# Block sums and early residual additions by accumulating transfers, and one seven-product pair of chunks in the first down pairs

## The chip, the cores and the metric

The kernel runs on one core of a Trainium2 chip. The metric is the device time of one execution in microseconds, as the median of several runs. The engines of the core are called here as the profile calls them: TensorE (PE), VectorE (DVE), ScalarE (ACT), GpSimd (POOL) and SyncE (SP). SP, ACT and POOL each have a queue from which they start DMA transfers.

## What is computed

A decoder trunk of two layers on 256 tokens of width 2048, all in float32. Layer 0 mixes tokens with gated linear attention, layer 1 with forgetting attention; both also attend to 256 memory tokens. The change touches the channel mixer, which each layer has after its attention, and two masks of the gated linear attention. The channel mixer of the reference:

```python
HIDDEN = 5632

def conv_ffn(h, w_up, conv_w, conv_b, w_down):
    u = causal_dwconv(h @ w_up, conv_w, conv_b)
    a, val = split_cols(u, [HIDDEN, HIDDEN])
    return (jax.nn.silu(a) * val) @ w_down

# in each layer, after the attention:
h = rmsnorm(x, norm_ffn[i])
x = x + conv_ffn(h, w_up[i], conv_w[i], conv_b[i], w_down[i])
```

## The kernel before

**Splitting.** A float32 matrix product is made of three fast products: each operand is split into a rounded high part (`whi`, made by ACT) and the rest (`wlo`, high part subtracted by VectorE), and hi·hi, hi·lo and lo·hi are added in PSUM. Weights arrive in units of 128 x 1024 floats (512 KB) on SP's queue into one of four `raw` buffers (`split_unit`, L212); `whi` and `wlo` have four buffers each. Activations (`h`, `m`) lie in SBUF already split, one buffer for each chunk of 128 rows.

**Pairs.** `pair_steps` (L351) multiplies all 256 tokens (two blocks of 128) by 1024 columns (two halves of 512) over n chunks. For one chunk that is 4 block products of 3 matmuls, 12 matmuls of 128 x 512, into four PSUM banks p2, p3, p4 and x. Some pairs of neighbouring chunks k, k+1 are done with **seven** block products instead of eight (Strassen's scheme in Winograd's form): 21 matmuls instead of 24. For those the tokens' sums stand ready (`token_sums`, L429; `usum`, `dsum`), and sums of the neighbouring weight blocks are needed: the two units come into `ra` and `rb` (tag raw2, two buffers), VectorE makes four sums of 128 x 512 (L397 to L400), and `split_more` (L342) casts four pieces w1 to w4 (512, 1024, 1024 and 1024 columns). Three more banks, p1, p5, p6 and p7, collect the products that several results share; after the last seven of a pair, `early` adds these into the results, and after the last unit `late` adds p2, p3, p4 and x.

**Channel mixer.** `ffn` (L330) works in parts of 16, 16 and 12 chunks of the hidden width (`PARTS`). *Up pairs* (11 in each layer, 16 units each) have a seven at chunk 6 (`SEVEN_UP`). Their `early` (L1417) puts the shared sums, scaled by the norm, into four temps; their results are turned from tokens to columns by a transpose on VectorE, a transfer to DRAM and four back on POOL's queue (`far_away`, L601). After a due time of 8 units (`turn(j, wait)`, L1386) the convolution's taps (ACT), their sums (VectorE), Silu and the product follow, two or fewer of these steps after each unit (`tick`). *Down pairs* multiply one part's gated chunks by 1024 of the 2048 output columns: f=0 for columns 0 to 1023 (x[0], x[1]), then f=2 (x[2], x[3]). In the first two parts both have sevens at chunks 4 and 10 (`SEVEN_DOWN`), so 8 sevens in each layer. A part's down pairs run after the first up pair of the next part. In the third part there are no sevens in the down product. The residual x lies in SBUF; `early` of a down pair (L1286) adds into it with one ACT and eight VectorE operations, four of which are additions to x (`add_to`, L453).

**Order.** A scheduler orders each engine's instructions by a simulated time line; `high_priority(offset=AHEAD)` lets an instruction be taken as if it stood 300 instructions earlier, which is how weights are loaded and split ahead. `issue_after` fixes an order by hand: all weight loads follow one another on SP's queue.

Of the kernel before, what the change touches and what calls it, by code (L numbers as in the profile page):

```python
# [20 lines left out]
P = 128  # L21
T = 256
# [13 lines left out]
SEVEN_DOWN = (4, 10)  # L36

# [107 lines left out]
def _trunk(ctx: ExitStack, tc: tile.TileContext, xt, xtok, memt, wp, wgu, gns, gfin, cnv, par, msk, out):  # L145
# [13 lines left out]
    mask = const.tile([P, M_N], F32, name="mask")  # L159
# [3 lines left out]
    scanmask = mask[:, M_SCAN : M_SCAN + T]  # L163
# [187 lines left out]
    def pair_steps(units, src, sums, flip, pool, early, late):  # L351
# [32 lines left out]
        places = (("p2", 0, 0), ("p3", 0, 1), ("p4", 1, 0), ("x", 1, 1))  # L384
        for k in plan:
            if k in sums:
                with tc.high_priority(offset=AHEAD):
                    ra, rb = [pool.tile([P, NUNIT], F32, name="raw2", tag="raw2", bufs=2) for _ in range(2)]
                    with tc.issue_after(loads[-1].ins):
                        for t, (off, _, w) in ((ra, units[k]), (rb, units[k + 1])):  # L390
                            loads.append(nc.sync.dma_start(t, wp[off : off + P * w].rearrange("(p n) -> p n", p=P)))
                st = [[sums[k][:, part, j, :] for part in range(2)] for j in (3, 0, 1, 2)]
                done = k == end[-1]
                w1 = split_more(ra[:, :512], 512)
                w2 = split_more(rb, 1024)
                with tc.high_priority(offset=AHEAD):
                    V.tensor_tensor(ra[:, :512], ra[:, 512:], ra[:, :512], ALU.subtract)  # L397
                    V.tensor_tensor(ra[:, 512:], rb[:, 512:], ra[:, 512:], ALU.subtract)
                    V.tensor_tensor(rb[:, 512:], rb[:, 512:], ra[:, :512], ALU.subtract)
                    V.tensor_tensor(rb[:, :512], rb[:, :512], rb[:, 512:], ALU.subtract)  # L400
# [12 lines left out]
                k += 1  # L413
            else:
                w = split_unit(units[k])
                last = k == n - 1
                steps = [(low, *place) for low in range(2) for place in places]
                if last:
                    steps.sort(key=lambda t: places.index(t[1:]))
                for low, name, b, h in steps:  # L420
                    for part in range(2 - low):
                        r = mm(name, tok(k, b)[part], w[low][:, h * 512 : (h + 1) * 512], last and low == 1)
                    if last and low:
                        ends.append(r)
                        late(b, h, bank[name])
                last_mm.append(r)
            yield k

    def token_sums(r, dst):  # L429

        t = r.rearrange("p s (b n) -> p (s b) n", b=2)
        a11, a21, a12, a22 = (t[:, n, :] for n in range(4))
        V.tensor_tensor(a22, a21, a22, ALU.add)
        V.tensor_tensor(a21, a11, a21, ALU.subtract)
        V.tensor_tensor(a11, a22, a11, ALU.subtract)
        V.tensor_tensor(a12, a12, a11, ALU.subtract)
        halves([dst[:, part] for part in range(2)], t)
# [272 lines left out]
    with tc.tile_pool(name="load", bufs=1) as lp:  # L710
# [57 lines left out]
        for u in range(8):  # L768
            step(u)
            if u == 1:  # L770
                squares()
            elif u == 3:
                for b in range(2):
                    S.activation(mv[0][:, b, :], mv[0][:, b, :], AF.Copy, scale=nrm.col()[:, b : b + 1])
                with tc.issue_after(loads[-1].ins):
                    for i in range(KC):
                        nc.sync.dma_start(xf[i], xt[i])
                    nc.sync.dma_start(part, par)
                    nc.sync.dma_start(mask[:, M_FOX:], msk[:, M_FOX:])
# [20 lines left out]
    def gla(nx):  # L800
        h, mix = bufB, bufA
        with tc.tile_pool(name="gla", bufs=1) as gp:
            scratch[0] = gp

# [28 lines left out]
            def gates(hd):  # L833
# [7 lines left out]
                for c in range(2):  # L841
# [11 lines left out]
                    V.tensor_tensor_scan(bc[:, c, :], scanmask, mz, 0.0, ALU.mult, ALU.add)  # L853
# [110 lines left out]
            def core(hd):  # L964
# [36 lines left out]
                eye = mask[:, M_EYE:].bitcast(I32).unsqueeze(1).to_broadcast(ins.shape)  # L1001
                V.copy_predicated(ins, eye, ps[:, 192:320].rearrange("p (b t) -> p b t", b=2))
                for li, B in enumerate(LEVELS):
                    H = B // 4
                    p3 = levels[li].rearrange("p (b c) -> p b c", b=2)
                    m3 = mask[:, M_LVL + NVER * li : M_LVL + NVER * (li + 1)].bitcast(I32)
# [276 lines left out]

    def down_pair(l, p, f, src, sums, flip, pool, temps, then=None):

        def early(bank):  # L1286
            t0, t1 = temps()
            S.activation(t0, bank["p1"], AF.Copy)
            add_to(f)(0, t0)
            V.tensor_tensor(t0, bank["p6"], t0, ALU.add)  # L1290
            V.tensor_tensor(t1, bank["p7"], t0, ALU.add)
# [38 lines left out]
    def ffn(l, nx, h, m, ys, zs, landing, then, pool, temps, spare=None, last=None):  # L1330
        with tc.tile_pool(name=f"ffn{l}", bufs=1) as fp:
# [79 lines left out]
            def up_pair(j):  # L1411

                count[2] += 1
                turns = [turn(j + 2 * h_, 8) for h_ in range(2)]
                u = {}

                def early(bank):  # L1417
                    u.update({(b, h_): temps(2 * b + h_) for b in range(2) for h_ in range(2)})
                    S.activation(u[0, 1], bank["p1"], AF.Copy)
                    S.activation(u[0, 0], bank["p1"], AF.Copy, scale=scale(0))  # L1420
                    V.tensor_tensor(u[0, 1], bank["p6"], u[0, 1], ALU.add)
                    V.tensor_tensor(u[1, 0], bank["p7"], u[0, 1], ALU.add)
                    V.tensor_tensor(u[0, 1], bank["p5"], u[0, 1], ALU.add)
                    V.tensor_tensor(u[1, 1], bank["p5"], u[1, 0], ALU.add)
                    for b, h_ in ((0, 1), (1, 0), (1, 1)):
# [22 lines left out]
            for p, (lo, hi) in enumerate(PARTS[:-1]):  # L1448
# [15 lines left out]
            wide = down_pair(l, p, 0, src, {}, 0, pool, lambda: (temps(0), temps(1)), then)  # L1464
# [61 lines left out]
    with tc.tile_pool(name="stash", bufs=1) as st:  # L1526
# [4 lines left out]
        with tc.tile_pool(name="turn1", bufs=1) as tp:  # L1531
            n2, then = preparing("kv", bufB, tp, dram, turned3, "raw2")
            ys = [const.tile([P, 4, 4, 2, 32], F32, name="yu", tag=tag) for tag in ("mk0", "mv0")]
            fixed = [vt.rearrange("p b t -> p (b t)")[:, 2048 + 512 * i : 2560 + 512 * i] for i in range(2)]

            def temps(i):
                return fixed[i] if i < 2 else tp.tile([P, 512], F32, name="temp", tag=f"temp{i}")
# [17 lines left out]
    with tc.tile_pool(name="store", bufs=1) as op:  # L1555
# [11 lines left out]
        def temps(i):  # L1567
            return op.tile([P, 512], F32, name="temp", tag=f"temp{i}")
# [116 lines left out]
```

## Time and profile before

| | us |
|---|---|
| median of 3 runs | 2282.79 |
| lowest, highest | 2279.04, 2285.32 |
| the profiled execution | 2282.04 |
| its span, first to last instruction | 2280.0 |
| TensorE busy | 2229.1 |
| VectorE busy | 1806.4 |
| ScalarE busy | 1421.8 |
| GpSimd busy | 127.0 |
| mean granted TensorE clock | 0.994 |

The matmuls of layer 0's channel mixer start at 457.6 us of the span, those of layer 1's at 1528.2. Rows of the profile name the line, the engine, the operation and the tiles (out<-in). A helper's line stands for all its calls, so L455 is every addition to x, and L229 and L348 are all splits. Tiles carry the name of the buffer that they lie in: `fvt` and `temp` are temps of the mixer, `mix`, `A`, `B` and `more` hold gated chunks, `yu` and `yzu` results on their way to being turned, `far` their place in DRAM. "PEld" is the load of a matmul's stationary operand.

### The profile page before, as it was taken

How to read it: one execution, taken by the hardware profiler on the slowest of the kernel's cores; microseconds unless marked ns; L12 is line 12 of the kernel's file. 1: busy time of each engine (PE TensorE's matmuls, PEld its weight loads, DVE VectorE, ACT ScalarE, POOL GpSimd, SP SyncE). 2: the span in 40 equal slices, each digit the busy share in tenths (PEclk: the TensorE clock that was granted, in tenths of full speed). 3: DMA queues.
4: the chain of work that ended last, by engine and by line, in shares of the span. 5: the costliest groups of instructions: out<-in, count | busy, mean ns of one | idle time of the engine just before them, and what ended most of it. 6: DMA issues, size and time to landing. Idle time of an engine off the chain costs nothing.

```text
span 2280.0 us, 30080 instructions
## 1 busy us (share of the span) xinstructions
PE 2229.1 (98%) x10311; PEld 1852.6 (81%) x10311; DVE 1806.4 (79%) x2667; ACT 1421.8 (62%) x2264; POOL 127.0 (6%) x239
## 2 busy tenths in 40 slices
PE   9999999999999999999999999999999999999997
PEld 7888888888887878778777998888787787878876
DVE  7768987688898878897777569677889878889776
ACT  6655665557776566764665455456776656775465
POOL 0000000001010001100100000000001001100010
PEclk9999999999999999999999999999999999999998
DMA  9866657876675667756678667676777556765674
GB/s 351 247 221 213 206 180 254 249 249 216 235 243 193 211 220 250 246 179 218 227 230 265 209 205 251 204 246 226 235 249 236 202 195 231 239 221 204 225 233 133
DMA packets 167170, 515.48 MB, mean 226 GB/s; under 512 B 20700, under 2 KB 43880, under 8 KB 167016
## 3 DMA queue, kind: packets, MB, share of 16 engines
q1 hardware_dynamic: 151080, 464.51, 62.1%
q0 software_dynamic: 15360, 48.25, 6.8%
q8 instruction: 81, 1.33, 0.2%
q10 hardware_dynamic: 576, 0.79, 0.1%
q14 instruction: 73, 0.60, 0.1%
HBM read 469.68 MB, written 43.79 MB: 225 GB/s over the span
## 4 chain that ended last, share of the span: by engine, by line
PE 75%; issue 11%; DVE 4%; ACT 4%; DMA 4%; POOL 1%; SPq 0%; ACTq 0%; DVEq 0%; POOLq 0%
PE acc L372 22%; PE acc L332 21%; PE ps_s L372 11%; PE ps_o L372 6%; PE ps_t L372 5%; PE acc L259 3%; PE acc L304 3%; PE ps_s L332 2%; PE acc L257 1%; DMA yzu<-far 1%; DMA raw<-wp 1%; ACT whi L228 1%; DVE wlo L229 1%; DVE wlo L348 1%; DMA fvt<-far 1%
## 5 line engine op out<-in xcount | busy, mean ns | idle before, releaser
L229 DVE TENSOR_TENSOR wlo<-raw,whi 128x1024 fp32r<-128x1024 f32 (+4 forms) x730 | 860.9, 1193 | 328.4 <-ACT whi L228 308.2
L228 ACT ACTIVATE whi<-raw 128x1024 fp32r<-128x1024 f32 (+4 forms) x730 | 743.1, 1036 | 443.4 <-PE acc L332 164.5
L332 PE MATMUL acc<-whi,B 128*128 128x512 f32 (+3 forms) x1264 | 297.1, 370 | 3.1 <-ACT B L496 2.3
L347 ACT ACTIVATE whi<-raw 128x1024 fp32r<-128x1024 f32 (+1 forms) x152 | 144.5, 953 | 218.3 <-PE acc L372 74.2
L332 PEld LDWEIGHTS acc<-whi,B 128*128 128x128 f32 x1264 | 229.8, 188 | 32.9 <-ACT B L496 3.3
L348 DVE TENSOR_TENSOR wlo<-raw,whi 128x1024 fp32r<-128x1024 f32 (+1 forms) x152 | 164.0, 1087 | 62.7 <-ACT whi L347 55.3
L372 PE MATMUL acc<-whi,B 128*128 128x512 f32 x792 | 202.9, 390 | 1.9 <-ACT whi L228 1.9
L372 PE MATMUL acc<-whi,mix 128*128 128x512 f32 x764 | 196.8, 391 | 2.3 <-ACT whi L228 2.3
L372 PEld LDWEIGHTS acc<-whi,B 128*128 128x128 f32 x792 | 148.2, 188 | 34.9 <-ACT whi L228 4.0
L372 PEld LDWEIGHTS acc<-whi,mix 128*128 128x128 f32 x764 | 142.8, 188 | 34.8 <-ACT whi L228 4.9
L332 PE MATMUL acc<-wlo,B 128*128 128x512 f32 (+3 forms) x632 | 161.3, 369 | 0.0
L332 PEld LDWEIGHTS acc<-wlo,B 128*128 128x128 f32 x632 | 116.1, 188 | 14.8
L1358 DVE TENSOR_TENSOR tap<-tap,tap 128x1024 f32<-128x1024 f32 x88 | 107.3, 1219 | 17.8 <-ACT tap L1350 12.9
L372 PE MATMUL acc<-wlo,B 128*128 128x512 f32 x396 | 111.9, 390 | 0.0
L372 PE MATMUL acc<-wlo,mix 128*128 128x512 f32 x382 | 108.4, 390 | 0.0
L372 PE MATMUL ps_s<-whi,mix 128*128 128x512 f32 x360 | 104.2, 401 | 0.0
L372 PE MATMUL ps_s<-whi,B 128*128 128x512 f32 x348 | 95.7, 391 | 0.0
L372 PEld LDWEIGHTS acc<-wlo,B 128*128 128x128 f32 x396 | 74.2, 188 | 16.0 <-DVE wlo L229 0.6
L372 PEld LDWEIGHTS acc<-wlo,mix 128*128 128x128 f32 x382 | 71.5, 188 | 15.7 <-DVE wlo L229 0.7
L372 PEld LDWEIGHTS ps_s<-whi,mix 128*128 128x128 f32 x360 | 70.1, 195 | 15.2
L372 PE MATMUL ps_o<-whi,mix 128*128 128x512 f32 x218 | 71.7, 402 | 10.0 <-ACT mix L485 8.9
L372 PEld LDWEIGHTS ps_s<-whi,B 128*128 128x128 f32 x348 | 65.6, 189 | 13.9
(497 smaller groups left out, 3898.1 us busy)
## 6 DMA issues: line engine op xcount, KB each, us to landing
raw<-wp SPq DMA_DIRECT2D x743, 512.0 KB, 4.5
raw<-wp SPq DMA_DIRECT2D x32, 384.0 KB, 3.5
far<-yu POOLq DMA_DIRECT2D x22, 512.0 KB, 6.0
fvt<-far POOLq DMA_DIRECT2D x88, 128.0 KB, 3.3
far<-yzu POOLq DMA_DIRECT2D x22, 512.0 KB, 6.0
yzu<-far POOLq DMA_DIRECT2D x88, 128.0 KB, 3.3
raw<-wp SPq DMA_DIRECT2D x24, 388.0 KB, 3.6
far<-blk SPq DMA_DIRECT2D x12, 512.0 KB, 5.0
```

The costliest lines, as they stand in the source:

```text
L228: casts.append(S.activation(hi[:, s], raw[:, s], AF.Copy))
L229: lows.append(V.tensor_tensor(lo[:, s], raw[:, s], hi[:, s].bitcast(F32), ALU.subtract))
L257: mm = TE.matmul(acc[p][c][:, :T], w[:, s], both[:, 0, :], start=False, stop=end and j == 3)
L259: mm = TE.matmul(acc[p][c], w[:, s], both, start=u == j == 0, stop=end and j == 3)
L304: mm = TE.matmul(acc[b][:, :n], src[kcs[j] - base][:, part, b * P : (b + 1) * P], w, start=u == 0 and low == part == j == 0, stop=u == end ...
L332: mm = TE.matmul(acc[b][:, :n], src[kc - base][:, part, b * P : (b + 1) * P], ready[low][:, j * n : (j + 1) * n], start=i == low == part = ...
L347: casts.append(S.activation(hi[:, :n], src, AF.Copy))
L348: lows.append(V.tensor_tensor(lo[:, :n], src, hi[:, :n].bitcast(F32), ALU.subtract))
L372: r = TE.matmul(bank[name], x, w, start=name not in begun, stop=last)
L1358: V.tensor_tensor(t, t, taps[n][:, :, :, :T], ALU.add)
```

## The change

- A seven's weight sums are no longer made by four VectorE operations on two loaded units. A new function `fetch` issues five transfers on POOL's queue: block a1 a2 into `ta`, a1 again into `first` (tag raw1, one buffer), block b1 b2 into `rb`; then, accumulating in SBUF, a2 is added to the first half of `ta` and b2 to its second half. VectorE makes the two sums that are left. Signs are turned round so that the sums need only additions (`token_sums`, `bank_sums`).
- `fetch(n7)` is called from four chunks before the seven on (`FETCH`), with the same 300 instructions of priority.
- `early` of down pairs: one ACT and four VectorE operations (`bank_sums`) leave the sums in two temps of 128 x 1024, and two accumulating transfers on POOL's queue add these to x[f] and x[f+1]. `early` of up pairs uses the same `bank_sums`, with four scalings instead of three and one copy from PSUM less.
- In down pairs with f=0 the pair of chunks at 4 is no longer a seven (8 products instead of 7); f=2 keeps both.
- The last up pair's steps are due after 5 units instead of 8.
- The part of the masks that only gated linear attention reads moves into a tile of its own, `gmask`, in that stage's pool, loaded on POOL's queue at the stage's start.

```diff
+FETCH = 4
...
         places = (("p2", 0, 0), ("p3", 0, 1), ("p4", 1, 0), ("x", 1, 1))
+        fetched = {}
+
+        def fetch(k):
+
+            (oa, _, w), (ob, _, _) = units[k], units[k + 1]
+            sa, sb = (wp[o : o + P * w].rearrange("(p n) -> p n", p=P) for o in (oa, ob))
+            with tc.high_priority(offset=AHEAD):
+                first = pool.tile([P, 512], F32, name="raw1", tag="raw1", bufs=1)
+                ta, rb = [pool.tile([P, NUNIT], F32, name="raw2", tag="raw2", bufs=2) for _ in range(2)]
+                nc.gpsimd.dma_start(ta, sa)
+                nc.gpsimd.dma_start(first, sa[:, :512])
+                nc.gpsimd.dma_start(rb, sb)
+                nc.gpsimd.dma_start(ta[:, :512], sa[:, 512:], accum_op=ALU.add)
+                nc.gpsimd.dma_start(ta[:, 512:], sb[:, 512:], accum_op=ALU.add)
+            fetched[k] = first, ta, rb
+
         for k in plan:
+            for n7 in end:
+                if n7 not in fetched and n7 - FETCH <= k:
+                    fetch(n7)
             if k in sums:
-                with tc.high_priority(offset=AHEAD):
-                    ra, rb = [pool.tile([P, NUNIT], F32, name="raw2", tag="raw2", bufs=2) for _ in range(2)]
-                    with tc.issue_after(loads[-1].ins):
-                        for t, (off, _, w) in ((ra, units[k]), (rb, units[k + 1])):
-                            loads.append(nc.sync.dma_start(t, wp[off : off + P * w].rearrange("(p n) -> p n", p=P)))
+                first, ta, rb = fetched[k]
                 st = [[sums[k][:, part, j, :] for part in range(2)] for j in (3, 0, 1, 2)]
                 done = k == end[-1]
-                w1 = split_more(ra[:, :512], 512)
+                w1 = split_more(first, 512)
                 w2 = split_more(rb, 1024)
                 with tc.high_priority(offset=AHEAD):
-                    V.tensor_tensor(ra[:, :512], ra[:, 512:], ra[:, :512], ALU.subtract)
-                    V.tensor_tensor(ra[:, 512:], rb[:, 512:], ra[:, 512:], ALU.subtract)
-                    V.tensor_tensor(rb[:, 512:], rb[:, 512:], ra[:, :512], ALU.subtract)
-                    V.tensor_tensor(rb[:, :512], rb[:, :512], rb[:, 512:], ALU.subtract)
+                    V.tensor_tensor(rb[:, 512:], ta[:, :512], rb[:, 512:], ALU.add)
+                    V.tensor_tensor(rb[:, :512], rb[:, :512], rb[:, 512:], ALU.add)
...
-                w3 = split_more(ra, 1024)
+                w3 = split_more(ta, 1024)
...
+    def bank_sums(bank, u):
+
+        S.activation(u[0, 0], bank["p1"], AF.Copy)
+        V.tensor_tensor(u[0, 1], u[0, 0], bank["p6"], ALU.subtract)
+        V.tensor_tensor(u[1, 0], bank["p7"], u[0, 1], ALU.add)
+        V.scalar_tensor_tensor(u[0, 1], bank["p5"], -1.0, u[0, 1], ALU.mult, ALU.subtract)
+        V.scalar_tensor_tensor(u[1, 1], bank["p5"], -1.0, u[1, 0], ALU.mult, ALU.subtract)
+
     def down_pair(l, p, f, src, sums, flip, pool, temps, then=None):
 
         def early(bank):
-            t0, t1 = temps()
-            S.activation(t0, bank["p1"], AF.Copy)
-            add_to(f)(0, t0)
-            V.tensor_tensor(t0, bank["p6"], t0, ALU.add)
-            V.tensor_tensor(t1, bank["p7"], t0, ALU.add)
-            add_to(f)(1, t1)
-            add_to(f + 1)(1, t1)
-            add_to(f + 1)(1, bank["p5"])
-            V.tensor_tensor(t0, bank["p5"], t0, ALU.add)
-            add_to(f + 1)(0, t0)
+            both = [temps(i) for i in range(2)]
+            bank_sums(bank, {(b, h): both[h][:, b, :] for b in range(2) for h in range(2)})
+            for h in range(2):
+                nc.gpsimd.dma_start(x[f + h], both[h], accum_op=ALU.add)
...
-                turns = [turn(j + 2 * h_, 8) for h_ in range(2)]
+                turns = [turn(j + 2 * h_, 5 if j + 4 == PARTS[-1][1] else 8) for h_ in range(2)]
...
-                    drive(down_pair(l, p, f, src, {c - lo: t for c, t in sums.items()}, count[2] % 2, pool,
-                                    lambda: (temps(0), temps(1))))
+                    now = {c - lo: t for c, t in sums.items() if f or c - lo > SEVEN_DOWN[0]}
+                    drive(down_pair(l, p, f, src, now, count[2] % 2, pool,
+                                    temps))
...
         with tc.tile_pool(name="gla", bufs=1) as gp:
             scratch[0] = gp
+            gmask = gp.tile([P, M_N - M_SCAN], F32, name="gmask")
+            nc.gpsimd.dma_start(gmask, msk[:, M_SCAN:])
```

More of the change, by code (lines that the diff above doesn't have):

```diff
@@ L852, in gates @@
                     V.tensor_tensor(mz, mz, e, ALU.subtract)
-                    V.tensor_tensor_scan(bc[:, c, :], scanmask, mz, 0.0, ALU.mult, ALU.add)
+                    V.tensor_tensor_scan(bc[:, c, :], gmask[:, :T], mz, 0.0, ALU.mult, ALU.add)
                 return bc
@@ L1413, in up_pair @@
                 count[2] += 1
-                turns = [turn(j + 2 * h_, 8) for h_ in range(2)]
+                turns = [turn(j + 2 * h_, 5 if j + 4 == PARTS[-1][1] else 8) for h_ in range(2)]
                 u = {}
                 def early(bank):
[L1418 to L1425, printed above, removed]
+                    both = [temps(i) for i in range(2)]
+                    u.update({(b, h_): both[h_][:, b, :] for b in range(2) for h_ in range(2)})
+                    bank_sums(bank, u)
+                    for b, h_ in ((0, 0), (0, 1), (1, 0), (1, 1)):
                         S.activation(u[b, h_], u[b, h_], AF.Copy, scale=scale(b))
```

22 lines of the change are left out of this document (11 added, 11 removed).

## The prediction

> **What bounds the kernel now.** I read the page's first part, then a table of stretches of 40 us through both channel mixers, then who waited for whom, then single stretches in order of time.
>
> ```profile
> span 2280.0 us, 30080 instructions
> PE 2229.1 (98%) x10311; PEld 1852.6 (81%) x10311; DVE 1806.4 (79%) x2667; ACT 1421.8 (62%) x2264; POOL 127.0 (6%) x239
> ```
>
> TensorE is busy all along, so a change pays only where TensorE stands still, or where it has fewer matmuls. The profiled execution took 2282.04 us, 2 us more than its span and 0.75 us under the median of the runs; I count from 2282.0. The stretches hold, per engine, busy time and instructions in brackets, then granted clock, DMA share and GB/s:
>
> ```profile
> 520.00:680.00 160.00, 158.86 (x694) 129.31 (x693) 138.64 (x169) 124.16 (x201) 16.55 (x30) 1.00 0.70 237
> 680.00:720.00 40.00, 35.15 (x143) 27.14 (x142) 33.64 (x41) 25.90 (x44) 5.51 (x10) 0.96 0.57 182
> 820.00:940.00 120.00, 118.55 (x518) 96.40 (x517) 100.39 (x122) 91.33 (x147) 15.42 (x28) 1.00 0.71 230
> 940.00:980.00 40.00, 35.02 (x150) 27.33 (x148) 34.83 (x45) 25.10 (x42) 5.51 (x10) 1.00 0.64 214
> 980.00:1020.00 40.00, 40.00 (x176) 32.67 (x175) 38.02 (x45) 25.52 (x36) 0.00 (x0) 1.00 0.60 211
> 1760.00:1800.00 40.00, 34.67 (x141) 26.99 (x141) 32.53 (x39) 28.69 (x46) 4.39 (x8) 0.96 0.54 158
> 2020.00:2060.00 40.00, 35.02 (x136) 26.39 (x135) 32.27 (x40) 26.33 (x45) 5.52 (x10) 0.91 0.60 184
> 2060.00:2100.00 40.00, 40.00 (x175) 32.63 (x174) 37.23 (x44) 22.54 (x26) 0.00 (x0) 1.00 0.57 198
> ```
>
> 680, 940, 1760 and 2020 us are where the first down pair (f=0) of a part runs; 980 and 2060 lie in second pairs (f=2). Undisturbed, 40 us hold 175 or 176 matmuls, 0.228 us each. The four first pairs hold 143, 150, 141 and 136, together 132 too few: 132 x 0.228 = **30 us of TensorE lost**. Its busy times there fall 20 us short of 160; the rest is that after a stall matmuls take longer (three of the four stretches have a granted clock of 0.91 to 0.96, and the first row below a maximum of 794 ns):
>
> ```profile
> L372 PE MATMUL acc<-whi,dsum x64: 390/397/794, 689.2 to 2095.4; 128*128 128x512 f32 x64
> PE acc L372 <- ACT whi L347: 18.2, 18, 2.2
> ACT whi L347 <- DVE raw L398: 51.1, 17, 4.9
> 711.75 1.06 ACT L347 ACTIVATE whi<-raw 128x1024 fp32r<-128x1024 f32 x1 [2.27 <-DVE raw L400]
> 712.86 0.73 PE L372 MATMUL acc<-whi,dsum 128*128 128x512 f32 x2 [1.70 <-ACT whi L347]
> ```
>
> The first row is duration min/median/max in ns; the next two are waits (total us, times, longest). TensorE waits for ACT's cast of a sum block, ACT for VectorE's subtraction (L398, L400). VectorE is late: it carries the sums, the early residual additions and the gating of the last up pair at once.
>
> **The change, part by part.** VectorE from 680 to 740 us, then its groups there, and the two casts over the run:
>
> ```profile
> 680.00:740.00 60.00, 53.14 (x66) 0.97 0.58 193
> L397 DVE TENSOR_TENSOR raw<-raw 128x512 f32<-128x512 f32 x3 | 2.1, 685 | 0.0
> L400 DVE TENSOR_TENSOR raw<-raw 128x512 f32<-128x512 f32 x3 | 2.1, 687 | 0.0
> L455 DVE TENSOR_TENSOR x<-x,fvt 128x512 f32<-128x512 f32 x4 | 2.7, 689 | 0.4 <-ACT fvt L1288 0.4
> L229 DVE TENSOR_TENSOR wlo<-raw,whi 128x1024 fp32r<-128x1024 f32 (+4 forms) x730 | 860.9, 1193 | 328.4 <-ACT whi L228 308.2
> L348 DVE TENSOR_TENSOR wlo<-raw,whi 128x1024 fp32r<-128x1024 f32 (+1 forms) x152 | 164.0, 1087 | 62.7 <-ACT whi L347 55.3
> ```
>
> (1) *One seven fewer in each of four first pairs.* Eight products of three matmuls replace seven: 4 x 3 x 0.228 = **+2.7 us** of TensorE, for certain. VectorE loses, per pair, four sums of 0.69 us and 4 x 1.09 - 2 x 1.19 = 2.0 us of casts: 4.7 us.
>
> (2) *Two sums instead of four in each seven left* (38 before, from L348's 152 casts; 34 after): 1.4 us each. Three sevens start between 680 and 740 us; two remain: 2.8 us.
>
> (3) *Four of early's eight VectorE operations become two transfers*: 4 x 0.69 = 2.8 us per pair.
>
> So VectorE's load there falls by 10.3 to 42.8 us, while TensorE has 60 less about 7.5 lost, plus 0.7, or 53 us of matmuls: 81%, under the 87% (138.64 of 160) of the stretch 520 to 680, where TensorE lost 1.1 us. The stall should go but for scheduling accidents; I leave 1.5 us in each pair: 30 - 6 = **-24 us**. Bounds: all of it (-30), and 15 if only the stall at the dropped seven goes.
>
> (4) *Sums fetched on POOL's queue.* Five transfers per seven, three plain and then two accumulating ones that wait for the first to land; the waiting POOL instruction holds back what follows on its queue, mostly the turning transfers of the up pairs. The trace has no accumulating transfer. Nearest rows (KB each, median us from issue to landing; duration of an issue on POOL; and the two moments that matter in an undisturbed second pair):
>
> ```profile
> raw<-wp SPq DMA_DIRECT2D x743, 512.0 KB, 4.5
> far<-yu POOLq DMA_DIRECT2D x22, 512.0 KB, 6.0
> fvt<-far POOLq DMA_DIRECT2D x88, 128.0 KB, 3.3
> mv1again<-parkmv POOLq DMA_DIRECT2D x1, 512.0 KB, 8.5
> L604 POOL DMA_DIRECT2D far<-yu x22: 533/558/561, 505.4 to 1131.1; - x22
> 739.63 1.62 SPq L391 DMA_DIRECT2D raw<-wp  x2
> 753.96 0.63 PE L372 MATMUL acc<-whi,dsum 128*128 128x512 f32 x2
> ```
>
> The tight place is the second seven of a second pair: its buffers come free at 739.6, the first product starts at 754.0, and the first block that needs an accumulated sum follows nine matmuls later, 756.0, less 1.1 us for its cast: 754.9. The first plain transfer lands at 739.6 + 6.0 = 745.6; both accumulating ones are issued by 746.8. They may take **8.1 us**. Bounds for 256 KB: 3.3 us (128 KB, plain) to 12 us (twice the 6.0 of 512 KB); I take 6, between 128 and 512 KB plus a second read of the destination, and so no wait; at 12 us it is 4 x 3.9 = 16 us. Everywhere else, by the order of the code, the buffers come free about ten units (10 x 12 x 0.228 = 27 us) before use. The Trainium skill, "Collectives: The Full Stack", section "The bandwidth ceiling: the fold count and why AG ≠ RS ≠ AR", says that an adding transfer is slower because it has two source reads, not because of the addition, which halves its rate; no run here shows it. By it 256 KB would cost what 512 KB cost in a copy, 6.0 us, and the sum stays as it is.
>
> (5) *Residual additions by transfer*: 512 KB each, in 8 down pairs. The late addition to the same x must now wait for them.
>
> ```profile
> 760.14 0.68 DVE L1291 TENSOR_TENSOR fvt<-ps_s,fvt 128x512 f32<-128x512 f32 x1
> 768.06 2.47 DVE L455 TENSOR_TENSOR x<-x,acc 128x512 f32<-128x512 f32 x4
> ```
>
> The first row is early's second addition; two more at that pace end near 764. With two issues, a landing after 8.5 us is at 773.5, 5.5 us after the late additions would start. VectorE then stands, and what queues behind it is the wlo of the next units; three of the four wlo buffers are full by then, 3 x 12 x 0.228 = 8.2 us of matmuls. So nothing at 8.5, and about 8 pairs x 1 us for each us beyond 11. I take 0; bounds 0 and 32 us (15 us landing).
>
> (6) *More bytes.* 34 x 1.75 MiB and 4 MiB against 38, and 8 for the residual: 33.5 MiB or 35 MB more.
>
> ```profile
> DMA packets 167170, 515.48 MB, mean 226 GB/s; under 512 B 20700, under 2 KB 43880, under 8 KB 167016
> ```
>
> That is 7%; the shares of 0.57 to 0.71 above leave room. For later weight loads and turns I add 3 us (0 to 8).
>
> (7) *Turns of the last up pair due after 5 units instead of 8.* Both mixers end with a stall:
>
> ```profile
> 2221.86 0.60 ACT L1349 ACTIVATE tap<-yzu,cw 128x256 f32<-128x256 f32 x1 [2.66 <-DMA yzu<-far]
> 2235.00 0.80 PE L372 MATMUL ps_o<-whi,mix 128*128 128x512 f32 x1 [4.89 <-ACT mix L485]
> ```
>
> The tap already starts the moment its transfer lands, so an earlier place cannot start it sooner; it can get Silu and the cast of mix ahead of weight casts, or hold weight casts behind a waiting tap. I take 0; bounds -9 (both stalls gone) and +10 (5 us each).
>
> (8) *The rest at nothing*: signs, the same five ACT and four VectorE operations in up's early, and gmask, loaded by POOL while the first panel of values runs; the scan that needs it comes after two panels. Uncovered it would cost 8.5 us once.
>
> Sum: 2282.0 + 2.7 - 24 + 3 = 2263.7, **2264 us**.
>
> **The rivals.** *Accumulation lands late* (slower). Place: POOL's queue in the second pairs and before the late additions; decides from 8.1 us landing for sums and 11 for residuals. At 12 and 14: 16 + 8 x 3 = 40 us on 2264, 2304. For it: a destination that must also be read, and one mover at 8.5 us without an addition. Against it: the median of 6.0.
>
> *The stall stays* (no change). VectorE is freed, but ACT, which carries casts, taps and now waits for transfers, keeps TensorE waiting: 2282.0 + 2.7 = 2285. For it: TensorE's own wait names ACT. Against it: ACT is busy only 25.9 of 40 us there, and its wait names VectorE.
>
> *More is gained*: the two stalls of (7), 9 us and their slow clock, and half of what up pairs lose (2.6 us in the 280 us shown, 8 in some 900): 2264 - 13 = 2251.
>
> **How the numbers follow.** Forecast 0.52, accumulation late 0.22, stall stays 0.12, more gained 0.14. This kernel's runs tell 0.3% (6.8 us) from no change. The forecast and the larger gain lie below 2276: faster 0.66; same 0.12; slower 0.22. The forecast's own range, from its residual stalls and (6) and (7), is 2252 to 2276. For 8 in 10 it runs from 2246, past the larger gain, to 2290, which takes in the stall that stays and a mild form of the late landing.
>
> **What would show it.** Right: stretches at the four first pairs with 165 matmuls or more in 40 us and a clock near 1.00; VectorE at about 1806 - 88 us (38 x 4 - 34 x 2 = 84 sums and 8 x 4 additions of 0.69 us, and 8 of casts); 12 more matmuls; accumulating transfers landing in 8 us or less. Wrong: ACT's casts of sums waiting for transfers in second pairs, VectorE's residual additions waiting for them, or ACT's taps waiting longer for turned blocks because POOL's queue stood.

## The result, and the profile after it

The changed kernel took 2294.37 us (median of 8 runs, 2289.92 to 2304.32) beside 2284.06 us (2277.68 to 2288.86) for the kernel before: ratio **1.0049, 95% interval [1.0026, 1.0072]**. It is slower by some 11 us where 2264 us, 18 to 20 us faster, was forecast. The profiled execution took 2295.79 us, its span 14.0 us more than before.

The page after, first part, DMA packets, DMA queues and DMA issues (columns as before):

```profile
span 2294.0 us, 30252 instructions
PE 2235.4 (97%) x10323; PEld 1856.2 (81%) x10323; DVE 1727.1 (75%) x2543; ACT 1414.1 (62%) x2256; POOL 258.6 (11%) x426
DMA packets 182067, 550.62 MB, mean 240 GB/s; under 512 B 22604, under 2 KB 45912, under 8 KB 181912
q0 software_dynamic: 40048, 119.35, 19.5%
raw<-wp SPq DMA_DIRECT2D x675, 512.0 KB, 4.8
raw<-wp POOLq DMA_DIRECT2D x102, 256.0 KB, 7.3
x<-temp POOLq DMA_DIRECT2D x12, 512.0 KB, 11.2
fvt<-far POOLq DMA_DIRECT2D x88, 128.0 KB, 4.8
```

What the change does is all there: 12 more matmuls, 124 fewer VectorE instructions (84 sums, 32 residual additions, 8 casts, just as counted) and 79 us less of its time, 35.1 MB more. But loads land later: the weights of plain units 4.8 us instead of 4.5, the turned blocks 4.8 instead of 3.3 (those that carry results out to be turned don't: 5.6 instead of 6.0). The waits (total us, times, longest) say who pays, after the change and, in the second fence, before it:

```profile
ACT whi L228 <- DMA raw<-wp: 189.7, 119, 4.9
ACT whi L347 <- DMA raw<-wp: 41.8, 9, 8.5
POOL raw L397 <- DMA raw<-wp: 97.9, 33, 7.6
DVE x L468 <- DMA x<-temp: 25.6, 12, 4.5
```

```profile
ACT whi L228 <- DMA raw<-wp: 51.6, 37, 4.1
```

ACT's casts of plain units waited 51.6 us for their weights before, and 189.7 us now. And the stretches (columns as in the prediction; after a few stalls the work stands some us later than before, so a first pair ends in the next row). The second fence has three of them in the kernel before:

```profile
680.00:720.00 40.00, 40.00 (x178) 33.04 (x177) 34.25 (x41) 28.84 (x48) 10.70 (x17) 1.00 0.80 241
720.00:820.00 100.00, 97.21 (x421) 78.21 (x420) 71.40 (x79) 47.46 (x53) 13.13 (x19) 1.00 0.82 253
940.00:980.00 40.00, 36.83 (x156) 28.94 (x155) 30.95 (x37) 26.92 (x43) 6.69 (x12) 0.98 0.65 218
1600.00:1760.00 160.00, 154.72 (x669) 125.68 (x668) 128.74 (x153) 122.66 (x200) 28.79 (x48) 0.99 0.80 249
1760.00:1800.00 40.00, 40.00 (x178) 33.00 (x177) 33.54 (x40) 28.67 (x49) 10.11 (x17) 1.00 0.75 230
1800.00:1900.00 100.00, 95.55 (x417) 77.58 (x416) 71.72 (x81) 48.92 (x56) 12.64 (x18) 1.00 0.82 250
2020.00:2060.00 40.00, 37.87 (x166) 30.76 (x165) 26.16 (x31) 26.30 (x45) 6.14 (x11) 1.00 0.73 240
```

```profile
720.00:820.00 100.00, 99.75 (x439) 81.79 (x438) 82.22 (x95) 50.99 (x58) 1.12 (x2) 1.00 0.64 219
1600.00:1760.00 160.00, 158.52 (x693) 129.07 (x691) 140.54 (x173) 118.58 (x192) 17.66 (x32) 1.00 0.72 243
1800.00:1900.00 100.00, 99.75 (x439) 81.88 (x438) 80.70 (x93) 48.66 (x53) 5.51 (x10) 1.00 0.68 231
```

The places where the first pairs stalled are partly mended (178 matmuls for 143, 178 for 141). But 720 to 820 and 1800 to 1900, whole before with 439 matmuls each, now have 421 and 417, and 1600 to 1760, up pairs, fell from 693 to 669. DMA's share of busy time there is 0.80 to 0.82, where it was 0.64 to 0.72.

Adding up what each matmul starts later than 0.227 us behind the one before it, where that is more than 0.15 us, gives TensorE's lost time (us) by place:

```
                            before   after
four first down pairs         29.4    21.1
first seven of each mixer      0.0     8.1
everywhere else               31.9    43.1
sum                           61.3    72.3
```

The 11.0 us more and 2.7 us for 12 matmuls make up the longer span. The middle row is a place that the prediction passed over. The timeline of the later mixer's first seven (start, us, engine, line, what; in brackets the idle time before it and its releaser; here and below rows in between are left out):

```profile
1541.53 0.53 POOL L394 DMA_DIRECT2D raw<-wp  x1 [79.39 <-DVE wlo L229]
1548.52 0.63 ACT L347 ACTIVATE whi<-raw 128x512 fp32r<-128x512 f32 x1 [8.51 <-DMA raw<-wp]
1551.85 1.22 PE L372 MATMUL acc<-whi,mix 128*128 128x512 f32 x2 [1.41 <-ACT whi L347]
1553.84 1.06 ACT L347 ACTIVATE whi<-raw 128x1024 fp32r<-128x1024 f32 x1 [1.56 <-DVE raw L412]
1554.95 1.21 PE L372 MATMUL ps_s<-whi,usum 128*128 128x512 f32 x4 [0.18 <-ACT whi L347]
```

GpSimd's queue issued the first load only at 1541.5, after a wait that ended with a split of the stage before on VectorE (L229); ACT stands 8.5 us for the first block, and TensorE behind ACT. The other new place is the late addition to x, behind the residual transfers:

```profile
1798.18 2.48 POOL L1314 DMA_DIRECT2D x<-temp  x2
1810.08 0.69 DVE L468 TENSOR_TENSOR x<-x,ps_o 128x512 f32<-128x512 f32 x1 [4.53 <-DMA x<-temp]
1811.95 1.20 PE L372 MATMUL acc<-wlo,mix 128*128 128x512 f32 x4 [2.77 <-DVE wlo L229]
1813.87 0.69 DVE L468 TENSOR_TENSOR x<-x,ps_s 128x512 f32<-128x512 f32 x1 [1.37 <-DMA x<-temp]
```

### The profile page after: what moved, and what is told of

Same layout as the page of the kernel before. It is cut to its first block, busy times and chain, and to the rows that moved or that the text cites. A ratio compares the mean times of both kernels' runs of the same rounds, so it can differ in the third digit from the quotient of the medians.

```text
span 2294.0 us, 30252 instructions
## 1 busy us (share of the span) xinstructions
PE 2235.4 (97%) x10323; PEld 1856.2 (81%) x10323; DVE 1727.1 (75%) x2543; ACT 1414.1 (62%) x2256; POOL 258.6 (11%) x426
## 5 line engine op out<-in xcount | busy, mean ns | idle before, releaser
L229 DVE TENSOR_TENSOR wlo<-raw,whi 128x1024 fp32r<-128x1024 f32 (+4 forms) x738 | 870.8, 1194 | 321.7 <-ACT whi L228 306.0
L228 ACT ACTIVATE whi<-raw 128x1024 fp32r<-128x1024 f32 (+4 forms) x738 | 752.1, 1036 | 510.7 <-DMA raw<-wp 189.7
L347 ACT ACTIVATE whi<-raw 128x1024 fp32r<-128x1024 f32 (+1 forms) x136 | 127.2, 948 | 181.9 <-PE acc L372 60.3
L348 DVE TENSOR_TENSOR wlo<-raw,whi 128x1024 fp32r<-128x1024 f32 (+1 forms) x136 | 145.8, 1088 | 84.7 <-ACT whi L347 81.9
L372 PE MATMUL ps_s<-whi,mix 128*128 128x512 f32 x384 | 109.0, 399 | 0.0
L372 PE MATMUL ps_o<-whi,mix 128*128 128x512 f32 x226 | 74.5, 402 | 13.7 <-ACT mix L498 8.3
```

The source lines that it names most:

```text
L228: casts.append(S.activation(hi[:, s], raw[:, s], AF.Copy))
L229: lows.append(V.tensor_tensor(lo[:, s], raw[:, s], hi[:, s].bitcast(F32), ALU.subtract))
L347: casts.append(S.activation(hi[:, :n], src, AF.Copy))
L348: lows.append(V.tensor_tensor(lo[:, :n], src, hi[:, :n].bitcast(F32), ALU.subtract))
L372: r = TE.matmul(bank[name], x, w, start=name not in begun, stop=last)
```

## The experiments

The theory at this point: the fetched sums cost more than they relieve, because they land late in front of casts. Its rivals: their traffic delays all other transfers; GpSimd's queue stands in front of the turned blocks; the residual transfers are what costs; and the relief of VectorE was never worth what was forecast. Ratios are to the kernel before on the same chip.

**The parts alone.** Three are the kernel before with one part each, the fourth has the fetched sums and nothing else.

```
drop_only:   now = {c - lo: t for c, t in sums.items() if f or c - lo > SEVEN_DOWN[0]}
resid_only:  nc.gpsimd.dma_start(x[f + h], both[h], accum_op=ALU.add)    # for add_to(...) x4
turn5_only:  turns = [turn(j + 2 * h_, 5 if j + 4 == PARTS[-1][1] else 8) for h_ in range(2)]
fetch_only:  after, with four add_to(...), all sevens, turn(j + 2 * h_, 8)
```

> Only the pair of chunks at 4 loses its seven in first down pairs; all sums stay on VectorE. Theory 'VectorE is late in the first pairs, and the change only put late transfers in its place': VectorE has 4.7 us less in each of four pairs, the stall at the dropped seven (3.6 us of about 7 in each) goes, 2.7 us of matmuls come, so 2284 - 14 + 3 = about 2273 us. Rival 'the stall of the first pairs is not VectorE's load' (ACT's taps and casts): about 2284 + 3 = 2287 us and the same stalls elsewhere in the pair.

> Only the residual additions of early become two accumulating transfers; sums as before. Theory 'late transfers': each lands after about 11 us, VectorE waits for it in the late additions for 3 to 5 us in most of eight down pairs, and gives back what its four operations saved: 2280 to 2290 us. Rival 'the residual transfers are harmless, the fetched sums do the damage': VectorE's 2.8 us less per pair show in the first pairs, 2272 to 2278 us.

> Only the due time of the last up pair's turns, 5 units instead of 8. Theory 'the landing of the turned blocks sets it': 2284 us within 3, the stall before the last chunks of each mixer keeps 4 to 5 us. Rival 'the due time sets it': both stalls go, 2274 us.

> Only the weight sums come by accumulating transfers on GpSimd's queue (with the moved masks and the changed signs); both sevens stay in first pairs, residual additions stay on VectorE, turns due after 8 units. Theory 'late transfers': the first seven of each mixer waits some 7 us in all, turned blocks and weight loads come later, while VectorE's two sums less per seven give little: 2288 to 2300 us. Rival 'the fetched sums are harmless, the residual transfers do the damage': 2270 to 2278 us, since VectorE has 1.4 us less at each of 38 sevens.

Measured: drop_only 2275.05 us, 0.9981 [0.9969, 0.9993]; resid_only 2277.58, 0.9992 [0.9979, 1.0004]; turn5_only 2280.69, 1.0000 [0.9987, 1.0013]; fetch_only 2302.06, **1.0094 [1.0072, 1.0116]**. The damage is the fetch; the due time does nothing, and the residual transfers alone, which land after 8.0 us, cost nothing. The dropped sevens gave 3.9 us, between the 11 of my theory and the loss of 3 of its rival.

**The fetch taken apart.** All four start from fetch_only.

```
fetch_copies:      nc.gpsimd.dma_start(ta[:, :512], sa[:, 512:])     # both without accum_op
                   nc.gpsimd.dma_start(ta[:, 512:], sb[:, 512:])
fetch_first_only:  without these two lines
fetch_sp:          loads.append(nc.sync.dma_start(...))              # ta, first, rb on SyncE
fetch_unread:      V.tensor_tensor(rb[:, 512:], first, rb[:, 512:], ALU.add)
                   w3 = split_more(rb, 1024)                         # nobody reads ta
```

> The kernel with only the fetched sums (2302 us against 2279 before, 1.0094), with its two accumulating transfers turned into plain writes to the same places, so that the two sums of the weights are left out of what is computed; bytes from memory, order and waits stay. If the adding itself is what costs (7.2 and 8.7 us to land, against 5 to 6 us for a plain one), the plain writes land in about 5 us, the chain ends some 5 us sooner and the time falls to 2285 to 2292. If the number of transfers, the wait of GpSimd's queue between the two steps and the 35 MB more are what cost, it stays within 4 us of 2302.

> The kernel with only the fetched sums, without the second step of the fetch: the two accumulating transfers are left out, and so the two sums of the weights; 26 MB less, and GpSimd's queue never waits for a landing between the steps. If the second step (its wait in front of the turned blocks, its bytes and its lateness) is the damage, 2302 us falls to 2270 to 2282, at or below the time before, since VectorE has two additions less in each seven than before. If the place of the loads on GpSimd's queue alone is the damage, it stays at 2295 to 2302.

> The kernel with only the fetched sums, with the three plain loads of each seven on SyncE's queue, behind the weight load that stands before them, and only the two accumulating transfers on GpSimd's. If the loads' waits for free buffers on GpSimd's queue (164.5 us in the changed kernel, in front of the turned blocks) are the damage, 2302 us falls to about 2285 to 2290. If the damage is the second step's own length and the bytes, it stays within 4 us of 2302; and it rises above 2306 if the loads, waiting for free buffers, hold up the weight loads behind them on SyncE's queue.

> The kernel with only the fetched sums (1.0094), whose accumulating transfers still run with all their waits on GpSimd's queue and all their bytes, but nobody reads what they land: the two blocks that held sums are computed from the blocks of the first step, so the sums are left out. If the late landing in front of the casts is what the adding costs, it falls to the level of the fetch without a second step, 1.001 to 1.003, 2282 to 2287 us. If the traffic that they make for the other transfers is what costs, it stays at 1.007 to 1.010, 2296 to 2303 us.

Measured: fetch_copies 2287.06 us, **1.0024 [1.0013, 1.0035]**; fetch_first_only 2282.20, 1.0008 [0.9998, 1.0017]; fetch_sp 2303.11, 1.0103 [1.0086, 1.0120]; fetch_unread 2298.72, **1.0081 [1.0067, 1.0095]**. With the same bytes from the same places in the program, turning the addition off takes 0.7% away, some 16 us. Leaving out the second step's bytes as well (19.9 MB, not the 26 of my expectation) takes only 0.16% more. GpSimd's queue isn't it: with the plain loads on SyncE the kernel is no faster, and in fetch_only the transfers that turn results leave the queue 0.4 us (out) and 0.6 us (back) on average after what they wait for (0.3 and 0.8 before). Lateness, my theory, did not show in the time either: when nobody reads the accumulated blocks, 0.13% goes, which is inside the noise, and the rest stays. That run is not the same kernel without the reading, though. In it GpSimd's queue waited 191.8 us for landings in front of its accumulating transfers (93.5 in fetch_only), and ACT's taps waited 18.8 us for turned blocks (8.3), so part of its loss may be another than fetch_only's. What the adding does can be read from the software queue's row (packets, MB, time as a share of 16 engines' span) of fetch_first_only, of fetch_copies, and of fetch_only:

```profile
q0 software_dynamic: 29424, 98.37, 13.8%
```

```profile
q0 software_dynamic: 35504, 118.30, 16.2%
```

```profile
q0 software_dynamic: 40368, 118.30, 18.8%
```

The spans are 2282.6, 2280.2 and 2293.9 us, so the queue's time is 315, 369 and 431 us. The same 19.9 MB cost 54 us of all 16 DMA engines when they are written and 116 us when they are added, about 2.1 times as much. The Trainium skill, "Collectives: The Full Stack", section "The bandwidth ceiling: the fold count and why AG ≠ RS ≠ AR", says of ReduceScatter, a collective, that its addition needs two source reads and that it so reaches about half of a copy's rate; these rows agree with the factor for an accumulating transfer, but no row here shows the second read.

By which way this costs TensorE time is not shown. By the sum of late starts used above, TensorE lost 62.7 us in fetch_copies, 77.0 in fetch_only and 75.4 in fetch_unread, in one execution of each. In the first seven of each mixer it lost 6.4, 10.2 and 6.9 us, so there the late landing for the reader itself costs; in the rest of the up pairs ahead of each mixer's first down pair 5.8, 10.0 and 13.7 us, much of it at weight casts that stand behind taps on ACT. So fetch_unread is rid of one loss and has more of another. ACT's waits for the weights of plain units grew from 89.8 to 112.5 us with the adding. The packets on the plain loads' own queue took no longer (1272 us of 16 engines in fetch_copies, 1255 in fetch_only), and the median landing hardly moved (4.5 and 4.6 us). One place in fetch_unread, where ACT's taps wait for a turned block and the weight casts stand behind the taps:

```profile
1601.36 0.60 ACT L1368 ACTIVATE tap<-yzu,cw 128x256 f32<-128x256 f32 x1 [4.19 <-DMA yzu<-far]
1604.85 0.49 ACT L1370 ACTIVATE tap<-yzu,cw 128x256 f32<-128x256 f32 x1
1605.25 1.04 ACT L228 ACTIVATE whi<-raw 128x1024 fp32r<-128x1024 f32 x1
```

ACT stands 4.2 us, then works through nine taps, and only then casts the weights; TensorE's next matmul came 4.7 us late at this one place. In the changed kernel ACT's taps waited 21.5 us for turned blocks, as against 8.2 before. But that is not the price of the adding: with plain writes in its place (after_copies, below) they waited 24.4 us in a kernel that is 13 us faster.

```profile
ACT tap L1367 <- DMA yzu<-far: 13.6, 8, 4.8
ACT tap L1367 <- DMA fvt<-far: 7.9, 8, 2.8
```

```profile
ACT tap L1349 <- DMA yzu<-far: 5.9, 4, 2.7
ACT tap L1349 <- DMA fvt<-far: 2.3, 4, 1.3
```

```profile
ACT tap L1367 <- DMA yzu<-far: 15.1, 8, 5.0
ACT tap L1367 <- DMA fvt<-far: 9.3, 7, 3.3
```

(The first fence is the changed kernel's waits, the second those of the kernel before, the third those of after_copies.)

**The whole change taken apart.**

```
after_copies:           after, both second-step transfers without accum_op
after_vector_residual:  after, with the four add_to(...) of down_pair's early
change_nofetch:         drop_only + resid_only, and of the four subtractions only
    V.tensor_tensor(rb[:, 512:], ra[:, :512], rb[:, 512:], ALU.subtract)
    V.tensor_tensor(rb[:, :512], rb[:, :512], rb[:, 512:], ALU.subtract)
```

> The changed kernel with its two accumulating transfers per seven turned into plain writes to the same places, so that the two sums of the weights are left out of what is computed; every other part, byte and wait of the change stays. Between the two kernels with only the fetched sums this turned 1.0094 into 1.0024. If the adding by the transfers is also what turned the whole change, 1.0049 becomes 0.997 to 0.999, 2274 to 2279 us beside 2281. If the residual transfers and the bytes carry it, it stays at 1.003 to 1.005, 2288 to 2293 us.

> The changed kernel with the four early residual additions of each down pair on VectorE again; the rest of the change stays. In the changed kernel VectorE waited 36 us for these transfers, whose landing took 11.2 us beside the fetched sums and 8.0 us without them. If that wait is part of the loss, 1.0049 falls to 1.001 to 1.003, 2284 to 2288 us beside 2281. If the wait is covered and VectorE's relief is worth more, it rises to 1.006 or above, 2295 us.

> The same two sums left out, with the dropped seven in the first pairs and the residual additions by transfers: all of the relief that the prediction counted on VectorE, without a fetched transfer. If the prediction's step from that relief to TensorE's stalls was right and the fetch alone spoiled it, 0.990 to 0.993, 2257 to 2264 us beside 2280. If that step was wrong by itself, 0.995 to 0.997, no better than with four sums (0.9966).

Measured: after_copies 2278.58 us, **0.9991 [0.9980, 1.0003]**; after_vector_residual 2293.02, 1.0057 [1.0045, 1.0069]; change_nofetch 2273.40, **0.9976 [0.9964, 0.9988]**. So the change is a ledger of three lines, in us of some 2280: relief of VectorE with the dropped sevens 0.9976, -5.5; the fetch as plain transfers 0.9976 to 0.9991, +3.4; the adding 0.9991 to 1.0049, +13. By their intervals the three are known to some 3, 4 and 6 us, so the first and the third are clear of noise and the middle one is not. Nor is it the same everywhere: with all sevens kept, the plain fetch takes 0.9969 (before_twosums, below) to 1.0024 (fetch_copies), +12.5. The residual transfers can't be told from nothing: 1.0057 without them lies inside the interval of 1.0049 with them, though VectorE waits 36 us for them. And change_nofetch lies just above the second of its two ranges: the step from relief to stalls was wrong by itself.

**VectorE's load.** Why is the relief worth 5.5 us and not 21? The kernel before, with none and with two of the four subtractions:

```
before_nosums:   without the four V.tensor_tensor(...) of ra and rb
before_twosums:  with the two lines of change_nofetch in their place
```

> The kernel before without VectorE's four subtractions in each seven, so that the sums of the weights are left out of what is computed; loads, casts and products stay. VectorE loses 38 x 4 x 0.69 = 105 us of work, 6.9 us at least in each first down pair, and the casts of the last two blocks no longer wait for it. If VectorE's load sets the stalls of the first pairs, as the prediction had it, 20 us or more go: 2260 us or less beside 2280, 0.991. If the order of the work in front of the casts and the landing of the weights set them, 0.995 to 0.999, 2269 to 2278 us.

> The kernel before with two of VectorE's four subtractions in each seven, so that two sums of the weights are left out of what is computed; the loads are those of before, and nothing is fetched in their place. All four left out gave 0.9876. If the stall follows VectorE's load, half of that: 0.993 to 0.995, 2264 to 2269 us beside 2280. If the casts of the last block still wait in the same chain (cast, subtraction, sum, cast), little goes: 0.997 to 1.000.

Measured: before_nosums 2252.17 us, **0.9876 [0.9861, 0.9892]**; before_twosums 2271.24, **0.9969 [0.9955, 0.9983]**. VectorE's sums do make the stalls, 28 us of them, but half the sums are worth a quarter of it. The timeline of before_twosums at the second seven of a first pair:

```profile
2037.89 1.22 DVE L1356 TENSOR_TENSOR tap<-tap,tap 128x1024 f32<-128x1024 f32 x1
2039.03 0.68 DVE L397 TENSOR_TENSOR raw<-raw,raw 128x512 f32<-128x512 f32 x1
2039.74 0.69 DVE L398 TENSOR_TENSOR raw<-raw 128x512 f32<-128x512 f32 x1
2040.53 1.06 ACT L347 ACTIVATE whi<-raw 128x1024 fp32r<-128x1024 f32 x1 [0.21 <-DVE raw L398]
2041.64 1.22 PE L372 MATMUL acc<-whi,dsum 128*128 128x512 f32 x2 [2.39 <-ACT whi L347]
```

The last cast still hangs on a chain: an addition of taps, two sums, the cast, then TensorE, which stood 2.4 us. Two sums fewer shorten it; they don't dissolve it. And where VectorE is early enough, the next queue takes over. In change_nofetch at the same seven:

```profile
2036.76 0.69 DVE L398 TENSOR_TENSOR raw<-raw 128x512 f32<-128x512 f32 x1
2037.38 0.50 ACT L1347 ACTIVATE tap<-yzu,cw 128x256 f32<-128x256 f32 x1
2040.36 0.49 ACT L1348 ACTIVATE tap<-yzu,cw 128x256 f32<-128x256 f32 x1
2040.76 1.04 ACT L347 ACTIVATE whi<-raw 128x1024 fp32r<-128x1024 f32 x1
2041.86 0.50 PE L372 MATMUL acc<-whi,dsum 128*128 128x512 f32 x1 [0.74 <-ACT whi L347]
```

The sum is ready at 2037.45, but ACT has taps of the last up pair in its queue and casts it 3.3 us later.

**Versions that could beat both.** Five compute the whole result. The first adds the two harmless parts, the next two shift the taps that stood in front of the cast, and the last two take both sevens out of the first pairs.

```
drop_resid:         drop_only + resid_only
best_turn13:        drop_resid, turn(j + 2 * h_, 13 if j in (16, 32) else 8)
best_turn4:         drop_resid, turn(j + 2 * h_, 4 if j in (16, 32) else 8)
plain_first:        before, now = {c - lo: t for c, t in sums.items()} if f else {}
plain_first_resid:  plain_first + resid_only
```

> The kernel before with two parts of the change and no fetched sums: the seven at chunk 4 left to plain blocks in the first pairs, and the early residual additions by accumulating transfers. The parts alone gave 0.9981 and 0.9992, so if they add up the ratio is 0.9973, 2273 us beside 2279. If they relieve the same stalls of the first pairs, it is no better than the better part, 0.998; if the late additions' wait for the transfers (11.2 us to land) is uncovered once the casts come sooner, 0.999 to 1.001.

> The kernel with the dropped sevens and the residual transfers and no fetched sums (0.9966), with the taps of the up pair that runs ahead of each part's first down pair due after 13 units instead of 8, so that they follow the second seven. Each first pair still loses 1.4 to 2.1 us of TensorE there, behind six taps on ACT in front of the last cast. If ACT's order is what sets that stall, it goes: 4 times 2 us, 2266 us beside 2281, 0.993. If the taps only stall another place, the second pair's first seven or the late additions, 0.996 to 0.999.

> The same kernel (0.9966) with those taps due after 4 units instead of 8, ahead of the second seven. If ACT's order sets the stall and the turned blocks have landed by then, the stall goes as with 13 units, 0.993. In the later mixer the taps were already waiting for their blocks (3.2 us), so there ACT would stand with casts behind it: then no better than 0.996, or worse, up to 1.000.

> The kernel before with plain blocks in place of both sevens in the first down pairs, which so have no early residual additions either: 24 matmuls more, 5.5 us; it computes the whole result. The four pairs lost 28.4 us. If the sevens' bursts of casts are what stalls there, most of that goes, 20 us or more: 2265 us or less beside 2280, 0.993. If the taps of the up pair that runs ahead stall plain blocks as well, half goes, 0.997 to 0.998; if nothing goes, 1.002.

> The same with the early residual additions of the second pairs, which keep their sevens, by accumulating transfers. These pairs lose little, so it should be within 0.001 of the one beside it; above 1.002 times that one if the late additions wait for the transfers in second pairs.

Measured: drop_resid 2273.22 us, 0.9966 [0.9957, 0.9976]; best_turn13 2278.21, 0.9993 [0.9984, 1.0003]; best_turn4 2273.23, 0.9966 [0.9955, 0.9978]; plain_first 2255.89, **0.9893 [0.9880, 0.9907]**; plain_first_resid 2257.16, 0.9902 [0.9889, 0.9916]. With 13 units the 2 us stalls moved into the first seven of the second pairs (2.8, 2.5, 2.7 and 1.5 us) and 1.6 us stayed in two first pairs; with 4 units the stalls of 2.1 us stayed in three of the four. The burst meets the taps here or elsewhere. What works is to take the sevens, their sums and the early residual additions away from the place where the taps fall due. The same four stretches in plain_first:

```profile
680.00:720.00 40.00, 39.90 (x176) 32.70 (x175) 28.70 (x31) 27.57 (x46) 5.50 (x10) 1.00 0.84 265
940.00:980.00 40.00, 38.66 (x170) 31.36 (x169) 27.00 (x29) 26.75 (x44) 5.50 (x10) 1.00 0.80 238
1760.00:1800.00 40.00, 39.69 (x174) 32.08 (x173) 33.41 (x38) 29.88 (x49) 0.00 (x0) 1.00 0.66 233
2020.00:2060.00 40.00, 40.00 (x176) 32.72 (x175) 32.92 (x37) 30.19 (x48) 0.00 (x0) 1.00 0.72 245
```

Read against before: 696 matmuls for 570, and the clock is 1.00 in all four (0.91 to 0.96 in three before), while VectorE is busy 122 us of the 160 (133 before) and ACT 114 (106 before). Its 24 matmuls more cost 5.5 us and it still gains 24.7.

## Why the prediction was wrong

**The step that failed first** is the one from (1), (2) and (3) to TensorE: VectorE's load in the stretch falls to 81% of TensorE's, so "the stall should go", -24 us, with the dropped seven's +2.7 a net -21.3 us. That relief without any fetch measured -5.5 us (-2.7 to -8.2 by its interval). The count of the removed instructions was right (VectorE's time fell by 79 us, not 88), and so was the cause it named for the stalls, VectorE's sums. The mistake was to turn a mean load over 60 us into a stall. A seven is a burst: cast, subtraction, sum and cast in a chain over three queues, in between taps and additions that are due at the same units. The chain is gone with no sums (0.9876) or no sevens (0.9893), and hardly shorter with half of the sums (0.9969). With the matmuls' 2.7 us taken out, the stalls gave back some 8 us, not 24, and little more than half of my lower bound of 15.

**The second is (4)**, the fetched sums at no wait. The accumulating transfers took 7.2 us (first) and 9.0 us (second, median by line), not 6, and the buffers are not free 27 us ahead everywhere: not in the first seven of each mixer, which lost 8.1 us. But the larger mistake is the term itself. I priced only how long the transfers take to land for their own reader, and set it to nothing. Adding instead of writing came to +13 us in the changed kernel (after_copies) and +16 in fetch_only (fetch_copies), with 2.1 times the DMA engines' time for the same bytes. I had half the rate in (4), and used it for the landing alone. How much of this is the reader's wait and how much comes over other transfers stays open, since fetch_unread changed more than its reader.

**(6)**, the bytes at +3 us, fits the 3.4 us of the plain fetch in the changed kernel, but that figure is inside its noise and the same step cost 12.5 us with all sevens kept, so the agreement may be luck. **(5)** took 8.5 us landing; it was 8.0 alone and 11.2 beside the fetch. That is past the limit of 11 us, and VectorE waited as foretold; at 1812 us of the changed kernel TensorE lost 2.8 us behind that wait. Yet the time without the transfers is no better; that VectorE's relief paid for the wait is a guess. **(7)** at nothing held: the due time alone gave 1.0000. **(8)** was not tried by itself.

**The rivals.** "Accumulation lands late" had the sign and the size nearly right (2304), but by luck. It put 16 us into the second pairs, which lost little, and 24 us into the late additions, whose transfers cost nothing that can be told from noise. "The stall stays" with ACT named as the next in line was the truer half of the answer, and I gave it 0.12 because ACT was busy only 25.9 of 40 us; being little busy on average didn't keep seven taps from standing in front of one cast. Of the signs that I named, the 165 matmuls were met in three stretches of four, though a part of the stalls had only moved into the next ones; landing in 8 us or less was met neither by the second transfer (9.0) nor by the residuals (11.2); and of the signs of a wrong prediction VectorE's wait for the residual transfers and ACT's for turned blocks showed (the latter without the adding too), while the casts of sums waited in the first sevens rather than in second pairs.

What stays open: fetch_first_only (1.0008) and before_twosums (0.9969) do the same two sums, so the first step of the fetch costs 0.4% by itself there; whether by its 10 MB, its place ahead of the units or its buffers was not tried apart. So does the way by which the adding reaches TensorE.

## What to carry to other kernels

Price a transfer by the DMA engines' time that it takes, not only by when it lands; the adding transfers here took 2.1 times that of writes. Work taken off an engine that is not full in the mean can cost more on the DMA side than it saves, even where the DMA engines are not full either (0.80 to 0.82 here). A stall in a burst is priced by the chain that sets it: leave the whole suspected work out once, then half of it, before trusting a share of load. Where a burst meets other work that falls due, it can be cheaper to do more arithmetic in plain form there (24 matmuls, 5.5 us) than to make the burst lighter.

## What the runs showed that was not expected

An accumulating write took about 2.1 times the DMA time of a plain write of the same bytes, with more packets on its queue (40368 for 35504), and turning writes into additions cost 0.6 to 0.7% of the kernel's time. By the profile, issuing the two additions of a seven kept GpSimd 0.88 and 1.22 us, issuing them as writes 0.54 us each. The residual transfers of 512 KB landed after 8.0 us without the fetched sums and 11.2 us beside them. The granted clock of 0.91 to 0.96 in three of the four first pairs was 1.00 in all four once their stalls were gone.
